# The first four products as one group, x past column 512 and the norm weights turned by VectorE and DRAM, and every block exchange in GpSimd's queue

## The chip, the cores and the metric

The kernel runs on one core of one Trainium2 chip. The metric is the device time of one execution in microseconds (us); lower is better. A core has TensorE (PE; its loading of the stationary operand is shown apart as PEld), VectorE (DVE), ScalarE (ACT), GpSimd (POOL) and SyncE (SP). Each engine works through its own instructions in order and waits for others by semaphores. DMAs are issued from the queues of SP, ACT or POOL, and share 16 DMA engines.

## What is computed

One decoder layer on 256 tokens of width 2048, in float32: a SwiGLU half, a token mixer of attention and a gated spatial branch, and a second SwiGLU half, each on the RMS-normed residual stream.

```python
x = x + 1/2 * swiglu(rmsnorm(x, ffn1_norm), ffn1_w_gate, ffn1_w_up, ffn1_w_down)
x = x + hybrid_mixer(rmsnorm(x, mix_norm), w_in, ...)
x = x + 1/2 * swiglu(rmsnorm(x, ffn2_norm), ffn2_w_gate, ffn2_w_up, ffn2_w_down)
return rmsnorm(x, final_norm)
...
def swiglu(x, w_gate, w_up, w_down):
    return (jax.nn.silu(x @ w_gate) * (x @ w_up)) @ w_down
```

The weights are read once: 2048 x 5632 for gate, up and down of each FFN, 2048 x 11776 for `w_in`, and three smaller ones.

## The kernel before

**Products.** Every matrix product is cut into columns of 512 (`NC`). A `gemm` is one such column block: 256 tokens (two tiles `t` of 128) by 512 columns, summed over `nk` blocks of 128 rows of the weight. Its two sums stand in two PSUM banks. Precision comes from splitting both operands in two float32r parts: the stationary side is `xhi` and `xlo` (transposed activations, 128 rows of the width by 256 tokens), the moving side is `wh` and `wl`. For each block of 128 rows and each `t` three products are made: wh by xhi ("hh"), wl by xhi ("hl"), wh by xlo ("lh").

**Units.** Weights come in units of four row blocks (1 MB, tile `raw`, three buffers), loaded by SP. A unit is two half units; the list `hus` holds all half units in the order of work, and the loop at the end runs through it by an index `i`. For each half unit ScalarE copies `raw` to `wh` (line 139) and VectorE subtracts to get `wl` (line 140); both have four buffers, so the splits of half unit `i` + 4 wait for TensorE to finish `i`. A half unit is 12 products on TensorE (line 149). `at(i, fn)` puts other work behind the products of half unit `i`, ahead of the splits of the half units that follow. So the order on every engine is written out by this loop.

**Order of half units.** `lay_out` takes the gemms one after the other; where a gemm has `pair`, it and the next one are interleaved so that the last unit of each comes at the end.

**The start.** x (256 x 2048) is not normed ahead: the products use x times the norm's weight, and 1/rms of each token is applied to the results. TensorE transposes x, 128 columns `k` at a time (`first_transposes`, line 235, two transposes each), ScalarE and VectorE evacuate it, scaled by the norm's weight, to `xhi` and `xlo` (`first_evac`, lines 239 and 240). This happens between the products of the first gemm, two `k` for each half unit ahead, laid out by hand in `begin`, `ready`, `early` and `midway`. SP loads x in five pieces between the first weights. The norm weights come as rows (`rows`), and TensorE transposes them to columns (`gcols`): the first 16 at the start, the other 44 at half unit 60 (`gains`).

**Block exchanges.** Everywhere else a transpose is done by `turn`: VectorE transposes blocks of 32 x 32 (`blocks`, line 191 or 197), one DMA writes 512 KB to DRAM (line 175), three half units later four DMAs of 128 KB read the blocks back, permuted (`back`, line 181), and `lag` (six or eight) half units after the first step the result is evacuated (`ev`). All five DMAs stand in SP's queue, between the weight loads. There are 49 such exchanges: the hidden activations of both FFNs, x after the first two parts of the layer, and those of the mixer.

Of the kernel before, what the change touches and what calls it, by code (L numbers as in the profile page):

```python
# [16 lines left out]
P = 128  # L17
S = 256
NT = S // P
# [22 lines left out]
def layer(ctx: ExitStack, tc: tile.TileContext, a, out):  # L42
# [25 lines left out]
    rows = sb.tile([60, P], F32, name="rows")  # L68
# [6 lines left out]
    load_rows(0, ACT)  # L75
    half = sb.tile([P, 2], F32, name="half")
# [3 lines left out]
    junk = sb.tile([P, NC], BF16, name="junk")  # L80
    DVE.memset(junk, 0.0)
# [12 lines left out]
    gcols = sb.tile([P, 60], F32, name="gcols")  # L94
# [6 lines left out]
    def gemm(w, c0, rows0, nk, lhs, post, pair=False):  # L101
        gemms.append(dict(w=w, c0=c0, rows0=rows0, nk=nk, lhs=lhs, post=post, pair=pair))


    def lay_out():
        i = 0
        while i < len(gemms):
            gs = gemms[i:i + 2] if gemms[i]["pair"] else gemms[i:i + 1]
            i += len(gs)
            units = [(g, u) for g in gs for u in range(g["nk"] // UK)]  # L110
            if len(gs) == 2:
                units.sort(key=lambda q: q[1] == q[0]["nk"] // UK - 1)
            for g, u in units:
                hus.extend([(g, u, 0), (g, u, 1)])
# [5 lines left out]

    def load_unit(i, parts=(0, 4)):
        g, u, _ = hus[2 * i]
        if i in raws:
            r = raws[i]
        else:
            r = raws[i] = big.tile([P, UK, NC], F32, tag="raw", bufs=RAWB, name=f"raw{i}")
        k0 = g["rows0"] + u * UK * P
        src = g["w"][k0:k0 + UK * P, g["c0"]:g["c0"] + NC].rearrange("(k p) c -> p k c", p=P)
        k = slice(*parts)
        SP.dma_start(r[:, k], src[:, k])  # L130
# [12 lines left out]
    def product(i, jj, t, kind):  # L143
        g, u, j = hus[i]
        if "ps" not in g:
            g["ps"] = [mm_bank(f"mm{i}_{q}") for q in range(NT)]
# [21 lines left out]
    def turn(i, name, q, put, dst, ev, lag=8):  # L168
        got = {}

        def blocks():
# [3 lines left out]
            SP.dma_start(m, d.rearrange("p j m b -> p j (m b)"))  # L175

        def back():
            got["e"] = e = dst()
            m = got["m"].rearrange("(i a) j r -> j a i r", a=32)
            for j in range(4):  # L180
                SP.dma_start(e[32 * j:32 * j + 32].rearrange("p (i r) -> p i r", i=4), m[j])

        at(i, blocks)
        at(i + 3, back)
# [47 lines left out]
    def first_transposes(k):  # L232
        b = first_banks[k] = first_banks.get(k) or tp_bank(f"xt{k}")
# [8 lines left out]
    def residual(e, n, c, banks, scale, norm):  # L242
# [16 lines left out]

        def evac(src):  # L260
# [7 lines left out]
        turn(e + (6 if c == 1 else 2), f"x{n}_{c}", 8, put_tokens(lambda: x[:, :, cs]),  # L268
# [537 lines left out]
    def ready(i, whole=False):  # L806
# [7 lines left out]
        if whole:  # L814
            split(i)
# [90 lines left out]
```

## Time and profile before

| | us |
|---|---|
| median of 3 runs | 2047.57 (2047.5 to 2048.29) |
| the profiled execution | 2047.7 |
| its span in the trace | 2046.0 |
| TensorE busy | 2035.8 |
| ScalarE busy | 974.5 |
| VectorE busy | 1182.3 |
| GpSimd busy | 12.5 |

Times in the trace count from the start of the span. The waits of an engine are given with what ended them; a DMA's time is from its issue to its landing. Matmuls are pipelined, so a product's own 0.38 us overlaps the next one; what counts is the distance from start to start. Lines of the kernel are named L and a number.

### The profile page before, as it was taken

The page shows a single profiled execution, that of the slowest core. Times are in us where ns is not written, and L with a number is a line of the kernel's source. Part 1 is how long each engine was busy: PE and PEld are TensorE (multiplying, and loading weights), DVE is VectorE, ACT ScalarE, POOL GpSimd, SP SyncE. Part 2 cuts the span into 40 slices and gives each one's busy share as a digit, 9 for nine tenths or more (in the row PEclk, how much of TensorE's full clock was granted, in tenths as well). Part 3 has the DMA queues.
Part 4 walks back from the last instruction along what each step waited for, and adds up shares of the span by engine and source line. Part 5 has one row for each costly group of instructions (what it writes and reads, how often), then busy time and mean ns, then how long its engine had stood idle before and what let it go on. Part 6 is the DMA issues. An engine that isn't in the chain of part 4 may idle for free.

```text
span 2046.0 us, 23823 instructions
## 1 busy us (share of the span) xinstructions
PE 2035.8 (100%) x9494; PEld 1781.4 (87%) x9494; DVE 1182.3 (58%) x1193; ACT 974.5 (48%) x1071; POOL 12.5 (1%) x18
## 2 busy tenths in 40 slices
PE   9999999999999999999999999999999999999998
PEld 7888888888888888888888888888888888888887
DVE  5555555455555657665665555565555555555554
ACT  6444444444445555455554444564444444444443
POOL 0000000000000000000000000000000000000000
PEclk9999999999999999999999999999999999999999
DMA  7776876566766855787766666776676656667664
GB/s 271 234 236 226 270 245 216 201 223 225 243 231 217 269 201 202 241 276 261 261 222 220 224 225 206 246 256 231 221 242 224 225 206 205 224 222 240 231 214 144
DMA packets 246775, 469.35 MB, mean 229 GB/s; under 512 B 11084, under 2 KB 38536, under 8 KB 246536
## 3 DMA queue, kind: packets, MB, share of 16 engines
q1 hardware_dynamic: 246344, 467.30, 68.8%
q8 instruction: 74, 1.21, 0.2%
q10 hardware_dynamic: 320, 0.53, 0.1%
q14 instruction: 37, 0.30, 0.0%
HBM read 439.22 MB, written 28.57 MB: 229 GB/s over the span
## 4 chain that ended last, share of the span: by engine, by line
PE 99%; issue 0%; ACT 0%; DVE 0%; POOLq 0%; POOL 0%
PE mm L149 98%; PE sp L458 0%; PE warm L772 0%; PE pv L624 0%; PE sc L587 0%; PE xt L235 0%; PE sc L585 0%; PE pv L620 0%; ACT x L740 0%; ACT xhi L239 0%; PE pv L621 0%; DVE x L725 0%; POOLq L901 0%; POOL rf L732 0%; ACT wh L139 0%
## 5 line engine op out<-in xcount | busy, mean ns | idle before, releaser
L140 DVE TENSOR_TENSOR wl<-raw,wh 128x1024 fp32r<-128x1024 f32 (+1 forms) x780 | 947.6, 1218 | 822.7 <-ACT wh L139 817.6
L139 ACT ACTIVATE wh<-raw 128x1024 fp32r<-128x1024 f32 (+1 forms) x780 | 817.9, 1052 | 1007.6 <-PE mm L149 976.7
L149 PE MATMUL mm<-wh,xhi 128*128 128x512 f32 x2144 | 814.0, 380 | 0.5 <-ACT wh L139 0.4
L149 PE MATMUL mm<-wh,xlo 128*128 128x512 f32 x2144 | 812.5, 379 | 0.0
L149 PE MATMUL mm<-wl,xhi 128*128 128x512 f32 x2144 | 811.8, 379 | 0.0
L149 PEld LDWEIGHTS mm<-wh,xhi 128*128 128x128 f32 x2144 | 405.2, 189 | 58.6 <-ACT wh L139 0.9
L149 PEld LDWEIGHTS mm<-wl,xhi 128*128 128x128 f32 x2144 | 405.4, 189 | 57.3
L149 PEld LDWEIGHTS mm<-wh,xlo 128*128 128x128 f32 x2144 | 405.2, 189 | 57.4
L149 PE MATMUL mm<-wl,hhi 128*128 128x512 f32 x704 | 266.8, 379 | 0.0
L149 PE MATMUL mm<-wh,hhi 128*128 128x512 f32 x704 | 266.8, 379 | 0.0
L149 PE MATMUL mm<-wh,hlo 128*128 128x512 f32 x704 | 266.8, 379 | 0.0
L149 PEld LDWEIGHTS mm<-wl,hhi 128*128 128x128 f32 x704 | 133.1, 189 | 18.9
L149 PEld LDWEIGHTS mm<-wh,hlo 128*128 128x128 f32 x704 | 133.1, 189 | 18.9
L149 PEld LDWEIGHTS mm<-wh,hhi 128*128 128x128 f32 x704 | 133.1, 189 | 18.9
L149 PE MATMUL mm<-wh,uT 128*128 128x512 f32 x192 | 58.0, 379 | 0.0
L149 PE MATMUL mm<-wh,mhi 128*128 128x512 f32 x128 | 48.5, 379 | 0.0
L149 PE MATMUL mm<-wl,mhi 128*128 128x512 f32 x128 | 48.5, 379 | 0.0
L149 PE MATMUL mm<-wh,mlo 128*128 128x512 f32 x128 | 48.5, 379 | 0.0
L149 PEld LDWEIGHTS mm<-wh,uT 128*128 128x128 f32 x192 | 36.3, 189 | 5.1
L149 PE MATMUL mm<-wl,uT 128*128 128x512 f32 x96 | 36.4, 379 | 0.0
L304 DVE SCALAR_TENSOR_TENSOR sg<-mm,rstd,sg 128x512 f32<-128x512 f32 x44 | 30.9, 743 | 0.0
L219 ACT ACTIVATE junk<-x 128x512 bf16<-128x512 f32 x30 | 18.9, 629 | 25.0 <-DVE x L247 18.6
(152 smaller groups left out, 600.6 us busy)
## 6 DMA issues: line engine op xcount, KB each, us to landing
raw<-in_w_in_dram SPq DMA_DIRECT2D x92, 1024.0 KB, 5.0
raw<-in_ffn_w_up_dram SPq DMA_DIRECT2D x88, 1024.0 KB, 5.1
raw<-in_ffn_w_down_dram SPq DMA_DIRECT2D x88, 1024.0 KB, 5.1
raw<-in_ffn_w_gate_dram SPq DMA_DIRECT2D x84, 1024.0 KB, 5.0
raw<-in_w_out_dram SPq DMA_DIRECT2D x16, 1024.0 KB, 5.1
raw<-in_w_sg_out_dram SPq DMA_DIRECT2D x12, 1024.0 KB, 5.7
bmh<-bth SPq DMA_DIRECT2D x22, 512.0 KB, 2.7
sg<-bmh SPq DMA_DIRECT2D x88, 128.0 KB, 4.9
```

The source lines that it names most:

```text
L139: ACT.activation(wh[:, k], r[:, k], AF.Copy)
L140: DVE.tensor_tensor(wl[:, k], r[:, k], wh[:, k].bitcast(F32), op=OP.subtract)
L149: PE.matmul(g["ps"][t], act[:, k, t * P:(t + 1) * P], in_turn(w[:, jj]), start=k == 0 and kind == "hh", stop=k == g["nk"] - 1 and kind == ...
L219: ACT.activation(junk, x[:, t, c * NC:(c + 1) * NC], AF.Square, accum_out=ss[n][:, t, c:c + 1])
L304: DVE.scalar_tensor_tensor(two(sg[:, t]), banks[t], rstd[:, t:t + 1], two(sg[:, t]), op0=OP.mult, op1=OP.mult)
```

## The change

Four edits go together.

1. **Order of the first four gemms.** `lay_out` now takes groups with bounds. The first four gemms (gate and up of the first two column blocks) are interleaved: half unit 0 of each (x columns 0 to 255), then half unit 1 of each (256 to 511), then half units 2 and 3 of each (512 to 1023), then the rest. Their eight sums stand in all eight banks of PSUM. A raw unit may now hold parts of two gemms.
2. **x past column 512.** TensorE transposes only `k` 0 to 3. The other three parts of 512 columns (`c` = 1, 2, 3) go through `turn`, at half units 1, 7 and 8. The last two loads of x are put off to half units 3 and 4.
3. **Norm weights.** The other 44 rows (and the biases in them) are transposed by VectorE in blocks and exchanged over DRAM by SP, at half units 32, 36 and 40.
4. **Block exchanges.** All five DMAs of every `turn` are issued from GpSimd's queue.

```diff
-    def turn(i, name, q, put, dst, ev, lag=8):
+    def turn(i, name, q, put, dst, ev, lag=8, read=3):
...
-            SP.dma_start(m, d.rearrange("p j m b -> p j (m b)"))
+            POOL.dma_start(m, d.rearrange("p j m b -> p j (m b)"))
...
-                SP.dma_start(e[32 * j:32 * j + 32].rearrange("p (i r) -> p i r", i=4), m[j])
+                POOL.dma_start(e[32 * j:32 * j + 32].rearrange("p (i r) -> p i r", i=4), m[j])
...
-        at(i + 3, back)
+        at(i + read, back)
...
+            steps = [(g, q) for g in gemms[i:i + size] for q in range(g["nk"] // 2)]
+            i += size
+            steps.sort(key=lambda s: sum(s[1] >= (b if b > 0 else s[0]["nk"] // 2 + b) for b in bounds))
+            hus.extend((g, q // 2, q % 2) for g, q in steps)
+
+    PAIR = (2, (-2,))
+    FIRST = (4, (1, 2, 4))
...
-    ffn(a["ffn1_w_gate"][0], a["ffn1_w_up"][0], a["ffn1_w_down"][0], down1, False)
+    ffn(a["ffn1_w_gate"][0], a["ffn1_w_up"][0], a["ffn1_w_down"][0], down1, FIRST)
...
-    load_unit(0, (1, 2))
+    for k in (1, 2, 3):
+        load_unit(0, (k, k + 1))
     load_x(S, NC)
-    load_unit(0, (2, 3))
-    load_unit(0, (3, 4))
-    for c in range(1, 4):
-        load_x(c * NC, (c + 1) * NC)
-        load_unit(c, (0, 2))
-        load_unit(c, (2, 4))
+    for k in (0, 1):
+        load_unit(1, (k, k + 1))
+    load_x(NC, 2 * NC)
+    for k in (2, 3):
+        load_unit(1, (k, k + 1))
+    load_unit(2)
...
-    def gains():
-        b = tp_bank("gc1")
-        PE.transpose(b[:, 0:60], rows, ident[0:60, 0:60])
-        DVE.tensor_copy(gcols[:, 16:60], b[:, 16:60])
...
+    def more_rows():
+        POOL.memset(rows[32:64], 0.0)
+        for i in range(1, 4):
+            load_rows(i)
+
+    def rows_out():
+        d = sb.tile([64, P], F32, name="gd")
+        DVE.transpose(d.rearrange("p (j b) -> p j b", b=32), rows.rearrange("p (j b) -> p j b", b=32))
+        xT["gains"] = m = dram.tile([64, P], F32, name="gm")
+        SP.dma_start(m, d)
+
+    def rows_back():
+        m = xT["gains"].rearrange("(i a) (j b) -> j a i b", a=32, b=32)
+        for j in range(4):
+            SP.dma_start(gcols[32 * j:32 * j + 32].rearrange("p (i b) -> p i b", i=2), m[j])
...
+    for c, i, lag, read in ((1, 1, 3, 1), (2, 7, 5, 3), (3, 8, 5, 3)):
+        turn_x(i, 0, c, lag, read)
+    for c in (2, 3):
+        at(c + 1, lambda c=c: load_x(c * NC, (c + 1) * NC))
...
+    split(0, slice(0, 1))
+    first_x((0, 1))
+    for i, k in ((0, 1), (1, 0), (1, 1), (2, 0), (2, 1)):
+        split(i, slice(k, k + 1))
     for i in range(n):
...
+        if i < n - LA - 1:
+            products(i, jjs=(0,), high_first=i < 4)
+            if i == 1:
+                first_x((2, 3))
+            products(i, jjs=(1,), high_first=i < 4)
         for f in callbacks.pop(i, []):
             f()
-        if i > 4:
-            advance(i + LA + 2)
+        if i > 0:
+            advance(i + LA + (2 if i > 1 else 0))
```

`turn_x` holds what `residual` did before: four scalings by the norm's weight on ScalarE (line 264 before, 273 now), one copy to `xhi`, and VectorE's subtraction to `xlo`.

On TensorE, before, in the second half unit of the program (mm0 is the first gemm, xt4 and xt5 the transposes of x columns 512 to 767):

```order
L149 MATMUL mm0_1_139<-wh1_161,xhi0_118 128x512
L149 MATMUL mm0_1_139<-wh1_161,xlo0_119 128x512
L149 MATMUL mm0_0_138<-wl1_162,xhi0_118 128x512
L149 MATMUL mm0_1_139<-wl1_162,xhi0_118 128x512
L235 MATMUL xt4_173<-ident_76,x_81 128x128 x2
L235 MATMUL xt5_176<-ident_76,x_81 128x128 x2
L149 MATMUL mm0_0_138<-wh1_161,xhi0_118 128x512
L149 MATMUL mm0_0_138<-wh1_161,xlo0_119 128x512
```

And now, in the second half unit, which belongs to the second gemm (mm1):

```order
L155 MATMUL mm1_1_161<-wl1_135,xhi0_115 128x512
L241 MATMUL xt2_168<-ident_76,x_81 128x128 x2
L241 MATMUL xt3_171<-ident_76,x_81 128x128 x2
L155 MATMUL mm1_0_160<-wh1_134,xhi0_115 128x512
L155 MATMUL mm1_0_160<-wh1_134,xlo0_116 128x512
L155 MATMUL mm1_1_161<-wh1_134,xhi0_115 128x512
```

These are the last transposes of x on TensorE now; before, five more such places follow.

On ScalarE, before, around the split of half unit 8 (wh8):

```order
L239 ACTIVATE xhi0_118<-xt15_292,gcols_84 128x256
L139 ACTIVATE wh7_299<-raw3_103 128x1024
L139 ACTIVATE wh8_321<-raw4_315 128x1024
L139 ACTIVATE wh9_325<-raw4_315 128x1024
L139 ACTIVATE wh10_343<-raw5_317 128x1024
```

And now; xt0_1 is the block of x columns 512 to 1023 read back from DRAM:

```order
L145 ACTIVATE wh7_246<-raw3_189 128x1024
L273 ACTIVATE xt0_1_210<-xt0_1_210,gcols_84 128x2x4x32 x4
L169 ACTIVATE xhi0_115<-xt0_1_210 128x1024
L145 ACTIVATE wh8_271<-raw4_215 128x1024
L145 ACTIVATE wh9_287<-raw4_215 128x1024
```

The evacuation of the exchanged block stands between the splits of half units 7 and 8.

On GpSimd, whose first work after the start was the power for the first norm (line 226 before), there stand now ahead of it:

```order
L181 DMA bmx0_1_187<-btx0_1_184 128x1024
L187 DMA xt0_1_210<-bmx0_1_187 32x4x256 x4
L181 DMA bmx0_2_324<-btx0_2_321 128x1024
L181 DMA bmx0_3_347<-btx0_3_344 128x1024
L187 DMA xt0_2_387<-bmx0_2_324 32x4x256 x4
L187 DMA xt0_3_412<-bmx0_3_347 32x4x256 x4
L232 TENSOR_TENSOR rstd0_436<-ms0_433,half_72 128x2
```

Before, none of its instructions was a DMA; now it issues 260.

More of the change, by code (lines that the diff above doesn't have):

```diff
@@ L75, in layer @@
     load_rows(0, ACT)
+    junk = sb.tile([P, NC], BF16, name="junk")
+    DVE.memset(junk, 0.0)
     half = sb.tile([P, 2], F32, name="half")
@@ L107, in lay_out @@
         while i < len(gemms):
[L108 to L114, printed above, removed]
+            size, bounds = gemms[i]["group"]
+            steps = [(g, q) for g in gemms[i:i + size] for q in range(g["nk"] // 2)]
[4 more added lines that the diff above has]
+    FIRST = (4, (1, 2, 4))
     def at(i, fn):
```

102 lines of the change are left out of this document (35 added, 67 removed).

## The prediction

> **What bounds the kernel now.** I read the page's busy times first, then its costliest groups, then the table of waits of TensorE, then the timeline of the first 25 us.
>
> ```profile
> span 2046.0 us, 23823 instructions
> PE 2035.8 (100%) x9494; PEld 1781.4 (87%) x9494; DVE 1182.3 (58%) x1193; ACT 974.5 (48%) x1071; POOL 12.5 (1%) x18
> ...
> PE 99%; issue 0%; ACT 0%; DVE 0%; POOLq 0%; POOL 0%
> ...
> L140 DVE TENSOR_TENSOR wl<-raw,wh 128x1024 fp32r<-128x1024 f32 (+1 forms) x780 | 947.6, 1218 | 822.7 <-ACT wh L139 817.6
> L139 ACT ACTIVATE wh<-raw 128x1024 fp32r<-128x1024 f32 (+1 forms) x780 | 817.9, 1052 | 1007.6 <-PE mm L149 976.7
> ```
> ```profile
> PE warm L772 <- DVE junk L81: 1.3, 1, 1.3
> PE mm L149 <- ACT wh L139: 0.4, 1, 0.4
> ```
>
> The chain that ended last is 99% TensorE. TensorE's own waits are two, 1.3 us before anything is there and 0.4 us once. ScalarE, in contrast, waits 976.7 us for TensorE to give a buffer back. So from about 25 us to the end nothing but the count of products sets the time, and only the start, an instruction more or less on TensorE, or a new wait can move it. The profiled execution took 2047.7 us, 1.7 us around its span, and stands 0.13 us above the median of 2047.57.
>
> ```profile
> 6.23 0.79 PE L149 MATMUL mm<-wh,xhi 128*128 128x512 f32 x1
> 7.20 0.63 ACT L139 ACTIVATE wh<-raw 128x512 fp32r<-128x512 f32 x1 [0.59 <-DMA raw<-in_ffn_w_gate_dram]
> 9.29 0.59 PE L149 MATMUL mm<-wl,xhi 128*128 128x512 f32 x2
> 10.25 0.48 PE L149 MATMUL mm<-wh,xhi 128*128 128x512 f32 x1 [0.36 <-ACT wh L139]
> 10.57 0.38 PE L149 MATMUL mm<-wh,xlo 128*128 128x512 f32 x1
> 11.21 0.59 PE L149 MATMUL mm<-wl,xhi 128*128 128x512 f32 x2
> 11.65 0.60 PE L235 MATMUL xt<-ident,x 128*128 128x128 f32 x4
> 12.00 0.46 PE L149 MATMUL mm<-wh,xhi 128*128 128x512 f32 x1
> 12.30 0.38 PE L149 MATMUL mm<-wh,xlo 128*128 128x512 f32 x1
> 30.04 0.38 PE L149 MATMUL mm<-wl,xhi 128*128 128x512 f32 x1
> 44.93 0.38 PE L149 MATMUL mm<-wl,xhi 128*128 128x512 f32 x1
> 168.17 0.38 PE L149 MATMUL mm<-wh,xlo 128*128 128x512 f32 x1
> 168.48 0.27 PE L785 MATMUL gc<-ident,rows 60*128 60x60 f32 x1
> 168.68 0.48 PE L149 MATMUL mm<-wh,xhi 128*128 128x512 f32 x1
> 169.00 0.38 PE L149 MATMUL mm<-wl,xhi 128*128 128x512 f32 x1
> ```
>
> Between 30.04 and 44.93 stand 69 products, 0.216 us each: that is the pace.
>
> **What is removed.** One visit of TensorE to four transposes: after two products from 11.21 the second next would start at 11.21 + 3 x 0.216 = 11.86; it starts at 12.30, so a visit costs **0.44 us**. Before there are seven visits after the first product, for x columns 256 to 2047; the order keeps the first of them (the same 256 columns, in the second half unit) and drops six: 6 x 0.44 = 2.64. The wait at 10.25: two products from 9.29 would be followed at 9.72 and 9.94, and the second came at 10.57: **0.63**. It comes because ScalarE has to evacuate x and split weights in turn; now four half units use the same 128-column blocks 0 and 1, and their weights' splits stand ahead of the next evacuation. The transposes of the norm weights: two products behind 168.17 would bring 168.60; it was 169.00: **0.40**. Their replacement (a 64-row transpose by VectorE, five small DMAs, a memset) lies at half units 32 to 40 behind VectorE's 822.7 us of idle time, and its result is used at the end of the first FFN, over 400 us later: 0. Without waits: 2047.7 - 2.64 - 0.63 - 0.40 = **2044.0**.
>
> The first product stays at 6.23: the first three loads are the same. The memset of junk goes ahead of two of 0.06 us: 0 to 0.1 gained, taken as 0. The loads that follow are the same bytes in an order nearer to their use, half of what x asked for is put off, and half unit 3 (due at about 15) sees its low part between 0.4 us early and 0.5 late: taken as 0.
>
> **What is added: the first block exchange, c = 1.** Half unit 8 is the first to use x columns 512 to 1023. It starts 90 products after the one that stood at 7.94 before, plus one visit: 7.94 + 19.4 + 0.5 = 27.9; its second product needs wl8, at 28.1. What must come before:
>
> ```profile
> GB/s 0 14 262 286 211 195 268 368 406 397 412 401 408 408 410 410 406 412 401 412 401 399 100 182 406 389 51 33 276 399 414 406 403 164 49 205 408 360 29 20
> L191 DVE STREAM_TRANSPOSE btx<-x 128x512 f32<-128x512 f32 x16 | 10.4, 687 | 0.0
> L239 ACT ACTIVATE xhi<-xt,gcols 128x256 fp32r<-128x256 f32 x16 | 7.0, 471 | 6.1 <-PE xt L235 6.1
> L264 ACT ACTIVATE xt<-xt,gcols 128x256 f32<-128x256 f32 x32 | 13.5, 494 | 1.3 <-DMA xt<-bmx 1.3
> L163 ACT ACTIVATE xhi<-xt 128x1024 fp32r<-128x1024 f32 x8 | 8.5, 1058 | 0.3
> L164 DVE TENSOR_TENSOR xlo<-xt,xhi 128x1024 fp32r<-128x1024 f32 x8 | 9.8, 1225 | 13.1 <-ACT xhi L163 13.1
> ```
> ```profile
> bmx<-btx SPq DMA_DIRECT2D x8, 512.0 KB, 2.8
> xt<-bmx SPq DMA_DIRECT2D x32, 128.0 KB, 4.8
> bmp<-btp SPq DMA_DIRECT2D x4, 512.0 KB, 4.1
> p<-bmp SPq DMA_DIRECT2D x16, 128.0 KB, 6.8
> k<-bmk SPq DMA_DIRECT2D x12, 128.0 KB, 8.0
> ```
> ```profile
> 648.50 1.75 SPq L181 DMA_DIRECT2D xt<-bmx  x4
> L226 POOL TENSOR_TENSOR rstd<-ms,half 128x2 f32<-128x2 f32 x3 | 2.1, 701 | 995.9 <-DVE ms L224 995.9
> L393 POOL TENSOR_TENSOR lnrs<-ve,half 128x2 f32<-128x2 f32 x1 | 1.6, 1595 | 60.7 <-DVE ve L391 60.7
> ```
>
> Each number of the first row is one us. The third load ends at 0.79 MB, moved by 5.1, and ScalarE began on it at 7.20, 2.1 later; the first load (0.26 MB) was moved by 2.9 and used at 3.7; I take 1.4 for the lag. Step by step: the second part of wh2 is the eighth piece (2.1 MB, moved by 9.2), lands at 10.6 and is split by 11.2; two evacuations of 0.47 on ScalarE, and VectorE's half of the last, bring 12.7; x columns 512 to 1023 (2.6 MB) are there at 11.9; two transposes of 0.687 end at **14.1**. Then one write of 512 KB to DRAM and four reads back, now issued by GpSimd. Then ScalarE, whose queue waits there with wh8 behind it: 4 x 0.494 + 1.058 for the block, 1.05 for wh8; VectorE does xlo (1.225), then wl8 (1.22). With T the last landing, wl8 is ready at T + 3.03 + 1.23 + 1.22 = T + 5.5. So the wait is **T - 22.6**, where positive.
>
> No row shows a DMA of GpSimd's. At SP's quiet prices the write takes 2.8, the fourth read is issued 1.3 after the first (1.75 for four) and lands 4.8 later: T = 14.1 + 2.8 + 1.3 + 4.8 = 23.0, a wait of 0.4. At the prices of the attention part's exchanges, 4.1 and 8.0: T = 27.5, wait 4.9. The first us row says which is nearer: 10 to 21 us moves 400 GB/s and more throughout, as full as any part, but GpSimd's queue has nothing queued ahead, where SP's had weights. I take the middle of the quiet and the busy prices (2.8 and 4.1; 4.8 and 6.8), T = 24.65. GpSimd's issue of one DMA I bound from 0.44 (SP's) to 1.6 (the dearer of its two-element operations) and take 1.0, not far from the 0.70 row; it adds 0.6 to the write and up to 1.7 to the reads, half of it beside transfers: 1.1. T = 25.8 and the wait is **3.2**, bounds 0 to 8.
>
> A rule that speaks against this edit: the Trainium skill, "DMA: Bandwidth & Descriptors", section "Latency and other measured facts", gives 0.6 us to the first byte for DMAs of SP and ScalarE and about 1 us for GpSimd's. No row here shows GpSimd's. By that rule T would be an estimated 0.8 later over the two legs, and the sum below 2049.3.
>
> **The second and third exchange, c = 2 and 3.** They are due at half units 16 and 18, the first of them 20.7 us after half unit 8, at 51.8. VectorE transposes them behind the splits of half units 10 and 11 (wl8 at 31.3, 1.22 for each split, 1.4 for each pair), done at 35.1 and 37.7. By the middle prices each takes 11.7 from there (25.8 - 14.1): c = 2 lands at 46.8, c = 3, whose reads stand behind those of c = 2, at about 51. ScalarE has 3.03 for c = 2, 1.05 for wh16, 3.03 for c = 3 and 1.05 for wh17, in this order; with VectorE's 1.23 and 1.22 behind each, wl16 is there at 52.3 (due 52.0) and wl17 at 56.5 (due 54.9): waits of 0.3 and 1.6. By the quiet prices both are in time, by the busy ones the two cost 3. The first row above has gaps from 22 us on (100, 51, 33, 164, 49), so this place is nearer to quiet than half unit 8 is; I take **1.3**, bounds 0 to 3.
>
> **The other 49 exchanges, moved from SP's queue to GpSimd's.** In SP's queue they held back weight loads; but the waits that this made ended at ScalarE, not at TensorE:
>
> ```profile
> ACT wh L139 <- DMA raw<-in_w_in_dram: 15.9, 9, 3.3
> ACT pTk L607 <- DMA p<-bmp: 0.9, 1, 0.9
> ```
>
> So nothing is won. Lost is nothing as long as the block arrives in its lag of six or eight half units (15.5 or 20.7 us) against 2.8 + 1.3 + 4.8 = 8.9; behind a waiting DMA on GpSimd stand only the next exchanges and the two-element powers for the norms, needed later. Taken as 0.
>
> **Sum:** 2044.0 + 3.2 + 1.3 = **2048.5 us**.
>
> **Rivals.** (A) All three exchanges come in time, since the queue of their own spares them the weights: T below 22.6, no wait, **2044.0**. For it speaks the wait of 0.4 at quiet prices, against it the 400 GB/s beside it. (B) Slower: an exchange by GpSimd costs more than SP's dearest. If each issue takes 1.6 and the landings are those of k<-bmk, T = 14.1 + 5.3 + 4.8 + 8.0 = 32.2, a wait of 9.6 at half unit 8, and of 3 at 16 and 17: 2044.0 + 12.6 = **2056.6**. It decides from waits of 3.7 on (all that is saved) and is measurable from 7.8 on. In such a wait TensorE is idle for long, and this case has a row of its slow pace, seven warm-up products in 3.17 us, 0.45 each where 0.216 is usual:
>
> ```profile
> 1.32 3.17 PE L772 MATMUL warm<-junk 128*128 128x512 bf16 x7 [1.32 <-DVE junk L81]
> ```
>
> The Trainium skill, "TensorE: Matmul & The Clock Gate", section "Part 1: The HAM clock gate", says that an idle window of about 3.4 us halves the clock until one busy window has passed. By that rule B would cost an estimated 1.7 us more (half of 3.4), 2058.3, and the forecast nothing, its wait being in parts (for wh8, then for wl8) that are shorter. (C) The move of the late exchanges does cost: the four of the attention part have no slack on ScalarE (the 0.9 above). Some 3 us more for each would reach TensorE's product with pT for about 1.5 each, 6 in all: **2054.5**. Against it: only those four are that tight.
>
> **How the numbers follow.** Forecast 0.5 (2045.5 to 2051.7), A 0.2, B 0.22, C 0.08. About 0.2%, 4.1 us, is what a measurement here can tell from no change. All that can be saved, 3.7, is less than that, so faster has 0.04 (A with the small gains at the start); the slower side is B, C and the edge of the forecast, 0.30; the same is 0.66. The range goes from A, 2044.0, to 2055, which leaves out the dear half of B.
>
> **What would show it.** Six visits fewer and no wait of TensorE before 27 us; at half unit 8 a wait of TensorE that ends with wl, with ScalarE waiting for the landing of xt; smaller ones at 16 and 17; the products otherwise 0.216 apart. Wrong would be: TensorE waiting earlier (weights late), no wait at all (A), or waits after 70 us (C).

## The result, and the profile after

The changed kernel takes **2060.56 us** (median of 6 runs, 2057.63 to 2062.73), the kernel before 2047.54 beside it: a ratio of **1.006**, 95% interval 1.0049 to 1.007. It is 13 us slower; the forecast was 2048.5, the range ended at 2055. The profiled execution took 2058.45, so it lies 2 us below the median, and its sum is made against the 2047.7 of before: 10.7 us to explain. The other 2 us of the median are not in this profile; what the runs show of them stands with e12.

Of the page after, the span, the shares of the chain that ended last, and TensorE's two groups of products with their idle time:

```profile
span 2056.6 us, 23906 instructions
...
PE 64%; DMA 2%; issue 1%; ACT 1%; DVE 1%; POOL 0%; POOLq 0%; ACTq 0%; DVEq 0%
...
L155 PE MATMUL mm<-wh,xhi 128*128 128x512 f32 x2144 | 814.6, 380 | 6.1 <-ACT wh L145 5.7
L155 PE MATMUL mm<-wl,xhi 128*128 128x512 f32 x2144 | 813.0, 380 | 3.9 <-DVE wl L146 3.9
```

TensorE waits 5.7 us for ScalarE's split and 3.9 for VectorE's, about 10 in all. Where they are is seen when the products are numbered: at the usual pace product N starts (N - 1) x 0.2158 us behind the first one. The start of product N, counted from the start of the span, less (N - 1) x 0.2158 is the time lost so far; it holds the time ahead of the first product too (6.23 us before, 5.87 after). Product 97 is the first of half unit 8, 145 the first of half unit 12, 300 the last of half unit 24. For the two kernels, in us:

| lost by product | 72 | 97 | 145 | 300 | 2900 | 3300 | 4000 |
|---|---|---|---|---|---|---|---|
| before | 10.40 | 10.40 | 10.40 | 10.41 | 10.89 | 10.91 | 15.17 |
| after | 6.90 | 11.85 | 15.63 | 19.33 | 19.42 | 20.98 | 25.86 |

(Between 3300 and 4000 other work of TensorE stands; it makes 4.26 before.) So the new order is 3.50 ahead at product 72, where 3.27 was forecast (2.64 + 0.63); 0.36 of the 3.50 is the earlier first product. Then 4.95 go at product 97, 3.78 up to product 145, 3.70 up to product 300 (all but 0.2 of it in three waits at half units 16 and 17), and 1.5 and 0.6 behind product 2900, at 700 to 735 us. The norm weights' 0.4 (10.41 to 10.89 before) are saved. In sum, from the unrounded starts, -3.50 + 4.95 + 3.78 + 3.70 - 0.39 + 1.54 + 0.62 = 10.7.

TensorE's timeline at half unit 8 (start, busy us, the wait in brackets), and the windows around it (busy us of PE, PEld, DVE, ACT and POOL with their counts, granted clock, share of the DMA engines, GB/s):

```profile
27.40 0.38 PE L155 MATMUL mm<-wh,xlo 128*128 128x512 f32 x1
32.57 0.80 PE L155 MATMUL mm<-wh,xhi 128*128 128x512 f32 x1 [4.79 <-ACT wh L145]
34.02 0.79 PE L155 MATMUL mm<-wl,xhi 128*128 128x512 f32 x1 [0.65 <-DVE wl L146]
34.60 0.63 PE L155 MATMUL mm<-wh,xlo 128*128 128x512 f32 x1
35.03 0.63 PE L155 MATMUL mm<-wh,xhi 128*128 128x512 f32 x1
```
```profile
30.00:32.00 2.00, 0.00 (x0) 0.00 (x0) 0.40 (x1) 1.97 (x4) 0.00 (x0) 1.00 0.61 238
32.00:34.00 2.00, 0.80 (x1) 0.29 (x1) 2.00 (x3) 2.00 (x3) 0.00 (x0) 0.54 0.02 8
...
36.00:38.00 2.00, 2.00 (x6) 1.56 (x5) 2.00 (x4) 0.72 (x2) 0.26 (x1) 0.50 0.80 203
38.00:40.00 2.00, 2.00 (x8) 1.68 (x7) 1.77 (x3) 0.89 (x1) 0.30 (x1) 0.75 1.07 422
40.00:42.00 2.00, 2.00 (x11) 1.74 (x10) 1.23 (x1) 1.78 (x6) 0.55 (x1) 1.00 0.90 330
```

The wait is 5.17 - 0.22 = 4.95 from product to product, then 1.45 - 0.22 = 1.23 for wl8. The granted clock is 0.5 from 32.2 to 39.0, and the products behind the waits stand 0.43 apart until 38.9: 2.55 more by product 145. What ScalarE and GpSimd did meanwhile, from their timelines:

```profile
28.78 1.70 ACT L273 ACTIVATE xt<-xt,gcols 128x256 f32<-128x256 f32 x4 [9.51 <-DMA xt<-bmx]
30.51 1.06 ACT L169 ACTIVATE xhi<-xt 128x1024 fp32r<-128x1024 f32 x1
31.47 3.88 ACT L145 ACTIVATE wh<-raw 128x1024 fp32r<-128x1024 f32 x4
...
53.17 1.71 ACT L273 ACTIVATE xt<-xt,gcols 128x256 f32<-128x256 f32 x4 [5.21 <-DMA xt<-bmx]
...
58.23 1.70 ACT L273 ACTIVATE xt<-xt,gcols 128x256 f32<-128x256 f32 x4 [1.31 <-DMA xt<-bmx]
```
```profile
14.07 0.73 POOL L181 DMA_DIRECT2D bmx<-btx  x1 [12.69 <-DVE btx L197]
19.73 2.19 POOL L187 DMA_DIRECT2D xt<-bmx  x4 [4.93 <-DMA bmx<-btx]
37.74 0.56 POOL L181 DMA_DIRECT2D bmx<-btx  x1 [15.82 <-DVE btx L197]
40.06 0.55 POOL L181 DMA_DIRECT2D bmx<-btx  x1 [1.76 <-DVE btx L197]
42.25 2.23 POOL L187 DMA_DIRECT2D xt<-bmx  x4 [1.63 <-DMA bmx<-btx]
50.11 2.22 POOL L187 DMA_DIRECT2D xt<-bmx  x4 [5.63 <-DMA bmx<-btx]
```

ScalarE's queue stands at the first evacuation for 9.51 us, with the splits of half units 8 to 11 behind it, all ready to run (3.88 us without a gap afterwards). The exchange begins when forecast, at 14.07, but its write lands 5.36 later and the last of its reads 7.30 behind its issue at 21.37: T = 28.67. The third exchange's write takes 9.37. In the first write's time, seen by DMA queue (packets, MB, share of 16 engines; q0 is GpSimd's, q1 SP's):

```profile
DMA packets 1024, 2.23 MB, mean 406 GB/s; under 512 B 62, under 2 KB 62, under 8 KB 1024
## 3 DMA queue, kind: packets, MB, share of 16 engines
q1 hardware_dynamic: 880, 1.71, 80.7%
q0 software_dynamic: 144, 0.52, 23.3%
```

The engines are full. The quarter that the exchange has of them is a mean of two parts: by the same view, from 14.1 to 16.3 no packet of q0 moves (q1 0.90 MB, 407 GB/s), and from 16.3 to 19 q0 has 47.4% of the engines and moves its 0.52 MB. The reads, issued from 19.73 on, are the same: no packet from 19.7 to 23.4 (q1 1.47 MB, 402 GB/s in all), then 0.52 MB by 28.7. The first packets start at 16.4 and 23.5, so some 6 of the 14.6 us are time in which nothing of the exchange moves while SP's loads do. Why they come so late isn't settled: beside 382 GB/s, reads issued at 658.5 had their first packet 1.5 us later. Of the 22 exchanges of the FFNs' hidden activations, in stretches of some 200 to 270 GB/s, the median write of the same 512 KB takes 3.3 in GpSimd's queue (2.7 in SP's before), and an issue is 0.55 us:

```profile
L187 POOL DMA_DIRECT2D sg<-bmh x88 | 48.6, 553 | 80.4 <-DMA bmh<-bth 71.0
...
bmh<-bth POOLq DMA_DIRECT2D x22, 512.0 KB, 3.3
sg<-bmh POOLq DMA_DIRECT2D x88, 128.0 KB, 4.1
```

### The profile page after: what moved, and what is told of

It reads as the page before. It is cut to its first block, busy times and chain, and to the rows that moved or that the text cites. A ratio compares the mean times of both kernels' runs of the same rounds, so it can differ in the third digit from the quotient of the medians.

```text
span 2056.6 us, 23906 instructions
## 1 busy us (share of the span) xinstructions
PE 2037.0 (99%) x9469; PEld 1779.9 (87%) x9469; DVE 1183.6 (58%) x1189; ACT 977.6 (48%) x1073; POOL 158.0 (8%) x279
## 4 chain that ended last, share of the span: by engine, by line
PE 64%; DMA 2%; issue 1%; ACT 1%; DVE 1%; POOL 0%; POOLq 0%; ACTq 0%; DVEq 0%
PE mm L155 63%; DMA xt<-bmx 1%; DMA bmx<-btx 1%; POOL xt L187 0%; DVE wl L146 0%; ACT xt L273 0%; PE sp L468 0%; PE pv L634 0%; PE sc L597 0%; ACT xhi L169 0%; PE sc L595 0%; DVE xlo L170 0%; PE pv L630 0%; ACT x L750 0%; DVE btx L197 0%
## 5 line engine op out<-in xcount | busy, mean ns | idle before, releaser
L181 POOL DMA_DIRECT2D bmh<-bth x22 | 12.4, 564 | 905.9 <-DVE bth L197 905.9
L187 POOL DMA_DIRECT2D sg<-bmh x88 | 48.6, 553 | 80.4 <-DMA bmh<-bth 71.0
L170 DVE TENSOR_TENSOR xlo<-xt,xhi 128x1024 fp32r<-128x1024 f32 x11 | 13.5, 1225 | 48.9 <-ACT xhi L169 48.9
```

Of the source, the lines that this page charges most:

```text
L170: DVE.tensor_tensor(lo, src, hi.bitcast(F32), op=OP.subtract)
L181: POOL.dma_start(m, d.rearrange("p j m b -> p j (m b)"))
L187: POOL.dma_start(e[32 * j:32 * j + 32].rearrange("p (i r) -> p i r", i=4), m[j])
```

## The experiments

The theory: the new order of products is the gain that it was thought to be, and all of the loss is exchanges that land after their evacuation is due on ScalarE, because they stand beside weight loads that SP's queue would have held back. Rivals: the new start itself is too tight, in any queue; GpSimd's queue is slow in itself; the slow clock is what costs. All kernels in one table, with the time lost by product as above (the fillers of e4 not counted); the ratio is to the kernel before, timed on the same chip.

| kernel | median us (runs) | ratio, 95% interval | 72 | 97 | 145 | 300 | 2900 | 3300 |
|---|---|---|---|---|---|---|---|---|
| e1 after, all on SP | 2054.54 (6) | 1.0021 to 1.0045 | 8.83 | 8.83 | 9.56 | 17.80 | 17.89 | 17.90 |
| e2 before, 49 on GpSimd | 2051.64 (10) | 1.0013 to 1.0031 | 10.13 | 10.13 | 10.14 | 10.14 | 10.62 | 12.45 |
| e3 after, evacuation later | 2056.14 (4) | 1.0027 to 1.006 | 6.73 | 10.49 | 12.95 | 13.20 | 13.29 | 15.24 |
| e4 after, filler | 2061.13 (4) | 1.0053 to 1.0083 | 6.90 | 12.77 | 13.39 | 20.11 | 20.19 | 22.55 |
| e5 after, 49 on SP | 2057.75 (4) | 1.0031 to 1.0061 | 7.02 | 11.72 | 15.93 | 21.11 | 21.20 | 21.21 |
| e6 slack, all on SP | 2051.80 (10) | 1.0007 to 1.0026 | 7.02 | 9.94 | 11.84 | 11.84 | 11.93 | 11.94 |
| e7 slack, first three on GpSimd | 2051.61 (10) | 1.0009 to 1.0028 | 6.54 | 10.44 | 12.59 | 12.60 | 12.69 | 12.70 |
| e8 as e2, evacuation later | 2047.41 (10) | 0.9988 to 1.0007 | 10.14 | 10.14 | 10.14 | 10.15 | 10.63 | 10.64 |
| e9 no first exchange | 2048.87 (11) | 0.9993 to 1.001 | 10.43 | 10.43 | 10.43 | 10.44 | 10.52 | 10.54 |
| e10 after, x loads later | 2063.20 (4) | 1.0056 to 1.0088 | 6.52 | 11.81 | 15.25 | 21.77 | 21.86 | 25.83 |
| e11 slack, all on GpSimd | 2050.57 (10) | 1.0002 to 1.0021 | 7.03 | 10.84 | 13.46 | 13.47 | 13.55 | 13.57 |
| e12 after again | 2058.47 (4) | 1.0041 to 1.0072 | 7.03 | 11.19 | 13.99 | 17.53 | 17.62 | 18.96 |
| e13 as e9, second visit later | 2046.22 (11) | 0.9985 to 1.0002 | 9.32 | 9.32 | 9.32 | 9.33 | 9.41 | 9.43 |
| e14 as e13, more warm-up | 2046.19 (11) | 0.9984 to 1.0001 | 8.97 | 8.97 | 8.97 | 8.98 | 9.07 | 9.08 |
| e15 as e13, visits earlier | 2044.99 (11) | 0.9977 to 0.9996 | 7.91 | 7.91 | 7.91 | 7.91 | 8.00 | 8.01 |

### e1: the changed kernel, all exchanges back in SP's queue

```diff
-            POOL.dma_start(m, d.rearrange("p j m b -> p j (m b)"))
+            SP.dma_start(m, d.rearrange("p j m b -> p j (m b)"))
...
-                POOL.dma_start(e[32 * j:32 * j + 32].rearrange("p (i r) -> p i r", i=4), m[j])
+                SP.dma_start(e[32 * j:32 * j + 32].rearrange("p (i r) -> p i r", i=4), m[j])
```

> The changed kernel, with all 52 exchanges back in SP's queue; the new start stays. Theory Q (the exchanges are late because on a queue of their own they share the DMA engines with weight loads that SP's queue would have held back): the write of the first exchange lands in about 2.8 us and the reads in about 5, T near 23 to 24, a wait at half unit 8 below 2 us, no slow pace of TensorE, no waits at 705 and 733 us: 2044 to 2047 us. Theory S (the start is too tight in either queue, since VectorE's transposes end at 14.1): the wait at half unit 8 stays above 4 us, or SP's waits make weights late before 27 us: 2054 us or more.

Half of theory Q came. SP's queue (timeline), ScalarE at the first evacuation, and TensorE at the later one:

```profile
15.32 0.34 SPq L181 DMA_DIRECT2D bmx<-btx  x1
...
18.45 1.76 SPq L187 DMA_DIRECT2D xt<-bmx  x4
```
```profile
25.14 1.70 ACT L273 ACTIVATE xt<-xt,gcols 128x256 f32<-128x256 f32 x4 [1.65 <-DMA xt<-bmx]
```
```profile
57.53 0.48 PE L155 MATMUL mm<-wh,xhi 128*128 128x512 f32 x1 [2.10 <-ACT wh L145]
```

The write lands 3.07 behind its issue (5.36 on GpSimd's queue) and the whole exchange takes 9.7 in place of 14.6, since SP issues the weights only behind it: 0.71 MB were moved in all from 15.3 to 18.5, against 2.23 in 5.5 us above. Half unit 8 loses 0.7, and the waits behind product 2900 go. But the second and third exchange are late here too (evacuated from 47.5 and 53.7; their writes, with weight loads ahead of them in SP's queue, took 5.7 and 4.6 us) and cost 8.2 us, a slow pace included. So the queue is a part, not the whole. The median, 2054.54, lies where theory S put it, but neither sign of S came: the wait at half unit 8 is short, and TensorE doesn't wait before 27 us. (In this run the first products stood 0.43 apart until 10.3 us, which is the 1.9 more at product 72.)

### e2 and e8: the 49 exchanges alone, and the slack that they need

e2 is the kernel before with only the queue changed, the same two lines as in e1 the other way round; e8 is e2 with one number more:

```diff
-        turn(e + (6 if c == 1 else 2), f"x{n}_{c}", 8, ..., evac, 6)
+        turn(e + (6 if c == 1 else 2), f"x{n}_{c}", 8, ..., evac, 8)
```

> The kernel before, with its 49 exchanges in GpSimd's queue and nothing else changed. Theory Q: the queue alone costs the waits seen at 705 and 733 us in the changed kernel, about 2 us: 2048.5 to 2051 us, the start as before. Theory N (the late exchanges cost nothing, as predicted; those two waits come from the shifted order): 2047 to 2048 us. If the queue is the dear part of the whole change: 2054 us or more.

> The kernel before with its 49 exchanges in GpSimd's queue, and the evacuation of the x exchanges 8 half units behind their start in place of 6. Landings stay as late as on GpSimd's queue with 6. Theory W (the cost is ScalarE's queue standing at an evacuation whose block has not landed, with splits behind it): the waits at 697 and 725 us go, 2047 to 2048.5 us. Rival (the load on the DMA engines itself costs, through late weights): 2050 to 2052 us as with 6.

e2 is 4.2 us slower than before, a little more than expected (3.2 in its profile, all of it at two places of TensorE, 697 and 725 us); e8 isn't slower at all. ScalarE's evacuations of x in the mixer's norm, in e2 and then in e8:

```profile
693.57 1.70 ACT L264 ACTIVATE xt<-xt,gcols 128x256 f32<-128x256 f32 x4 [4.49 <-DMA xt<-bmx]
...
721.14 1.71 ACT L264 ACTIVATE xt<-xt,gcols 128x256 f32<-128x256 f32 x4 [5.65 <-DMA xt<-bmx]
```
```profile
692.86 1.69 ACT L264 ACTIVATE xt<-xt,gcols 128x256 f32<-128x256 f32 x4
...
718.98 1.69 ACT L264 ACTIVATE xt<-xt,gcols 128x256 f32<-128x256 f32 x4
```

The last of these exchanges took 13.8 us in e2 from the issue of its write (707.22) to its last landing (721.04), and 13.3 in e8 (704.25 to 717.52). This transfer is nearly as slow in e8 (the one before it took 11.3 in place of 13.3); what went is the place in ScalarE's queue where splits had to stand behind it. The load on the DMA engines alone costs nothing here.

### e5: the changed kernel, only the first three exchanges on GpSimd's queue

```diff
         got = {}
+        queue = POOL if name[:3] == "x0_" else SP
```

> The changed kernel with GpSimd's queue for the first three exchanges only; the other 49 back in SP's. Theory Q (the 49 cost 3 to 4 us, as they did in the kernel before): the waits behind 690 us go, the start stays as in the changed kernel (a wait of about 6 us at half unit 8, slow pace, waits at 16 and 17): 2060.6 - 4 = 2056.5 us, within 1.5. Rival (the 49 were dear only with the old start): 2059 us or more. If all of the loss came from the 49: about 2047.

The loss at 700 to 735 us is gone (21.20 to 21.21 between products 2900 and 3300), and so is 2.8 of the median, a little less than expected; the start is at least as bad as in the changed kernel (21.11 lost by product 300 in place of 19.33, with the clock at 0.5 a second time, from 63.6 to 67.0).

### e3: the first evacuation two half units later

```diff
-    for c, i, lag, read in ((1, 1, 3, 1), (2, 7, 5, 3), (3, 8, 5, 3)):
+    for c, i, lag, read in ((1, 1, 5, 1), (2, 7, 5, 3), (3, 8, 5, 3)):
```

> The changed kernel, with the evacuation of the first exchange two half units later in the queues, so that the splits of half units 8 and 9 stand ahead of it on ScalarE and VectorE. T stays at about 28.7. Theory W (the wait is T plus what stands on the two engines behind the landing): half unit 8 starts at T + 2.8 = 31.5 in place of 32.6 and the second wait of 1.2 us goes: 2.3 us less, the slow pace stays since TensorE is still idle for 4 us: about 2056 (profile) to 2058 (median). Rival: wait falls below what slows TensorE and another 2.6 us go: 2053.5. Rival: the DMA is all that counts and nothing changes.

T stays (28.26), the time falls by 4.4. At half unit 8 TensorE now waits for the block itself:

```profile
31.21 0.48 PE L155 MATMUL mm<-wh,xhi 128*128 128x512 f32 x1 [3.60 <-ACT xhi L169]
31.53 0.38 PE L155 MATMUL mm<-wl,xhi 128*128 128x512 f32 x1
32.47 0.79 PE L155 MATMUL mm<-wh,xlo 128*128 128x512 f32 x1 [0.56 <-DVE xlo L170]
```

The loss between products 72 and 145 falls from 8.73 to 6.22, by 2.5 where 2.3 was expected, but not by the expected parts alone: half unit 8 starts 1.2 earlier relative to the pace (1.1 expected), the second wait falls by 0.5 (1.2 expected), and the slow pace, expected to stay, costs 0.8 less, since the clock is at 0.5 for 3.4 us in place of 6.8. The last part can be chance: see e12. More is won behind it: the transposes of the second exchange stand on VectorE behind the splits of half units 8 to 10, so its write goes out at 35.06 in place of 37.74, and half units 16 to 20 lose 0.25 in place of 3.70. One late landing makes the next.

### e4: products of zeros in the wait

```diff
+            if i == 8:
+                bank = hus[8][0]["ps"][0]
+                for _ in range(28):
+                    PE.matmul(bank, junk[:, 0:P], junk, start=False, stop=False)
```

> The changed kernel, with 28 products of zeros (6 us of TensorE) ahead of half unit 8, added into a running sum. TensorE is busy while it would wait. Theory C (after a long idle time TensorE runs at half pace for 5 us, 10 products at 0.43 in place of 0.216): the landing and the start of half unit 8 stay within 0.3 us, the granted clock stays 1.0, the products behind are 0.216 apart and the time falls by up to 2.6 us. Rival (the pace is hidden by the splits of half units 8 to 11, which keep ScalarE and VectorE fully busy until 36 us): waits for wl take its place, and the time falls by less than 1 us.

The clock holds (windows), the next products are at full pace, and the time is the same, 2061.13; TensorE's timeline shows where it goes:

```profile
32.00:34.00 2.00, 2.00 (x10) 0.83 (x8) 2.00 (x2) 2.00 (x3) 0.00 (x0) 1.00 0.04 14
34.00:36.00 2.00, 1.84 (x9) 1.60 (x9) 2.00 (x3) 2.00 (x4) 0.00 (x0) 1.00 0.00 0
```
```profile
34.75 0.38 PE L155 MATMUL mm<-wh,xhi 128*128 128x512 f32 x1
34.97 0.38 PE L155 MATMUL mm<-wl,xhi 128*128 128x512 f32 x1
...
61.24 0.48 PE L155 MATMUL mm<-wh,xhi 128*128 128x512 f32 x1 [1.42 <-ACT wh L145]
62.68 0.80 PE L155 MATMUL mm<-wl,xhi 128*128 128x512 f32 x1 [0.96 <-DVE wl L146]
```

By product 145 the kernel is 2.2 ahead of the changed one; by product 300 it is 0.8 behind. The second exchange lands at 51.8, only 1.2 earlier than in the changed kernel, and TensorE is there 2.2 earlier: four waits at half units 16 and 17 make 4.9 where three made 3.5, and behind the last of them the slow pace comes after all, for 1.6. The fillers also end late: half unit 8 starts at 33.49 in place of 32.57, and the wait for wl8 falls from 1.23 to 0.51. So both theories fail here: the clock's 2.2 us were won, and given back at the next landing.

### e10: less beside the first exchange?

```diff
-        at(c + 1, lambda c=c: load_x(c * NC, (c + 1) * NC))
+        at(5, lambda c=c: load_x(c * NC, (c + 1) * NC))
```

> The changed kernel, with the loads of x columns 1024 to 2047 (1 MB, first used at 36 us) one weight load later in SP's queue. Theory D (the first exchange is late because its packets share some 400 GB/s with everything SP has issued): 1 MB less stands beside the reads for about 2.5 us, T goes from 28.7 to between 26.5 and 28 and the wait at half unit 8 falls with it: 1 to 2 us less, 2058.5 to 2060. Rival G (GpSimd's queue itself is slow, its landings do not depend on what else moves): T stays within 0.3 us and the time within 1 us of 2060.6. Rival: the weights take the room that x leaves (the 1 MB that is moved ahead is as large), and T does not move either.

T = 28.63: it doesn't move. The weight load that changed places with x is as large, so the run doesn't tell late packets beside full engines from a slow queue. e1, and the 3.3 us of the same write in a quiet stretch, speak against the slow queue. The median, 2063.20, is above all that was expected: half units 16 to 20 lose 6.5 in place of 3.7, the mixer's norm 4.0 in place of 1.6, and behind both the clock is at 0.5 once more.

### e6, e7, e11: slack for all three exchanges

Three kernels with these two edits; all exchanges in SP's queue (e6), the 49 in SP's (e7), or all in GpSimd's and `lag` 8 as in e8 (e11).

```diff
-    FIRST = (4, (1, 2, 4))
+    FIRST = (4, (1, 2, 4, 6))
...
-    for c, i, lag, read in ((1, 1, 3, 1), (2, 7, 5, 3), (3, 8, 5, 3)):
+    for c, i, lag, read in ((1, 1, 5, 1), (2, 7, 7, 3), (3, 8, 11, 3)):
```

> The changed kernel with three edits that give the landings time: all exchanges in SP's queue; evacuations of the first three 2, 2 and 6 half units later, so that splits stand ahead of them; a bound more in the first group, so that the third exchange is needed at half unit 24 in place of 18. Theory W (only landings that come too late cost, and the new order of products is itself a gain of 3.5 us): no wait of TensorE from 12 to 100 us above 1 us, the time 2044 to 2046 us, below before. Rival S (the slow clock of the first products, 10.3 us in the run on SP's queue against 5.9 before, belongs to the new order): 2047 to 2049.

> As the one before it, but with GpSimd's queue for the first three exchanges, SP's for the others. Theory Q+W: T of the first exchange stays near 28.7, so a wait of about 3.5 us stays at half unit 8, with the slow pace or without it, and the other two exchanges cost nothing: 2048 to 2051 us. If GpSimd's queue is harmless once there is slack: equal to the one before it within 1 us.

> The changed kernel with all its exchanges and queues, only with slack: evacuations of the first three 2, 2 and 6 half units later, the third needed at half unit 24, the x exchanges of the later norms with 8 half units. Theory W: only the wait for the first exchange is left, 3.5 us at half unit 8 and the slow pace behind it, 1.5 to 2.5: 2047.6 - 3.9 + 5.5 = 2049.2 us, between 2048 and 2050.5, with no waits from 100 us on. Rival: waits elsewhere take their place, 2051 or more.

The second and third exchange cost nothing in any of them (the columns 145 and 300 agree), nor do the later 49 in e11. What is left is half unit 8: 6.4 us in e11 (1.9 of it slow pace), 6.1 in e7 (1.4), and 4.8 in e6. So e6 misses its range by 6 us; e7, 2051.61, and e11, 2050.57, end just above theirs. In e6 the block is there early and the weights aren't; ScalarE's timeline:

```profile
25.92 2.00 ACT L145 ACTIVATE wh<-raw 128x1024 fp32r<-128x1024 f32 x2 [3.51 <-DMA raw<-in_ffn_w_gate_dram]
27.83 1.69 ACT L273 ACTIVATE xt<-xt,gcols 128x256 f32<-128x256 f32 x4
```

SP's queue gives the exchange the bandwidth and takes it from the weights; GpSimd's does it the other way round. From 10 to 24 us the engines move some 400 GB/s, and 1 MB more of exchange has to come from somewhere. (e6 loses some 3 us more at 870 to 885 us, where ScalarE waits for weights, 16.7 us in six waits, and e7 0.8; this wasn't followed up.)

### e9, e13, e15: TensorE turns the first of the three parts after all

If the first exchange can't be in time, it has to go. All eight banks are taken from half unit 3 on; so the fourth gemm begins at half unit 6, and one bank is free until then for x columns 512 to 1023. All other exchanges stay in GpSimd's queue, with the slack of e11. The core of it:

```diff
+            if size == 4:
+                steps[0:8] = [steps[k] for k in (0, 1, 2, 4, 5, 6, 3, 7)]
...
-        b = first_banks[k] = tp_bank(f"xt{k}")
+        b = tp_bank(f"xt{k}") if k < 4 else first_banks["spare"]
+        b = first_banks[k] = b[:, (k % 2) * S * (k > 3):]
...
-    for c, i, lag, read in ((1, 1, 3, 1), (2, 7, 5, 3), (3, 8, 5, 3)):
+    for c, i, lag, read in ((2, 7, 7, 3), (3, 8, 11, 3)):
...
             if i == 1:
                 first_x((2, 3))
+                first_banks["spare"] = tp_bank("xt4")
+            if i in (3, 4):
+                first_x((2 * i - 2, 2 * i - 1))
```

e13 moves the second visit behind half unit 4, e15 both: the first to the middle of half unit 2, the second behind half unit 3.

> The first exchange is taken out: x columns 512 to 1023 are turned by TensorE, in half units 3 and 4, through a PSUM bank that is still free because the fourth product of the group now starts at half unit 6 in place of 3. The second and third exchange stay in GpSimd's queue, with their evacuations later and the third needed at half unit 24; all exchanges stay in GpSimd's queue, those of x with 8 half units. Theory W: no wait at half unit 8; the two visits of TensorE cost 0.9 us of the 3.5 gained; nothing else is lost: 2047.6 - 3.5 + 0.9 - 0.4 = 2044.6 us, between 2043.5 and 2046. Rival (weights are the next to be late, since 400 GB/s are in use until 25 us): waits of ScalarE for raw turn into waits of TensorE before 30 us, 2047 or more.

> As the kernel in which TensorE turns x columns 512 to 1023, with the second of its visits behind half unit 4 in place of in its middle, so that it doesn't wait for the bank (0.5 us there). With the release of the clock at 4.5 to 6.9: 2047.4 - 2.0 - 0.5 = 2045 us; with a release at 10.3: 2047. The median tells which is the more usual: below 2046, or 2047 and above as the 2048.9 of the kernel it is made from.

> As e13, with the two visits of TensorE in the middle of half unit 2 and behind half unit 3, so that the first evacuation stands ahead of the splits of half units 4 to 6. If the wait of 1.2 us came from the order in ScalarE's queue, it goes and nothing takes its place: 2046.2 - 1.2 = 2045.0 us, between 2044.6 and 2045.6, the kernel before at 2047.6. Rival (the weights that come at 17.7 us are the bound there, with 400 GB/s in use): TensorE waits for the splits of half units 4 to 6 instead, 2046 us or more.

No wait at half unit 8 is left in any of them. e9 is no faster than before and misses its range (2043.5 to 2046); its profiled run, 2047.40, has the slow first products of e1 (1.9 us). Its eleven runs fall in two groups, five of 2047.2 to 2047.9 and six of 2048.9 to 2049.6, and what parts them wasn't settled. e13, 2046.22, lies between its two forecasts: the slow first products are not there, but the second visit waits for the bank longer than in e9 (1.19 in place of 0.46), and the bank waits for an evacuation behind a split whose weights come at 17.9 (ScalarE, then TensorE):

```profile
17.98 1.06 ACT L147 ACTIVATE wh<-raw 128x1024 fp32r<-128x1024 f32 x1 [1.50 <-DMA raw<-in_ffn_w_up_dram]
18.95 0.46 ACT L248 ACTIVATE xhi<-xt,gcols 128x256 fp32r<-128x256 f32 x1
20.73 0.47 ACT L248 ACTIVATE xhi<-xt,gcols 128x256 fp32r<-128x256 f32 x1 [1.32 <-DVE xlo L249]
```
```profile
21.77 0.66 PE L244 MATMUL xt<-ident,x 128*128 128x128 f32 x4 [1.19 <-DVE xlo L249]
```

With the evacuation ahead of that split the wait goes and nothing takes its place. e15's visits on TensorE:

```profile
13.50 0.60 PE L244 MATMUL xt<-ident,x 128*128 128x128 f32 x4
...
17.82 0.60 PE L244 MATMUL xt<-ident,x 128*128 128x128 f32 x4
```

**e15 beats both kernels**: 2044.99 us against 2047.87 of before beside it, ratio 0.9986 (0.9977 to 0.9996), as expected. (The changed kernel was timed on other chips: 2060.56 and, in e12, 2058.47.)

### e12 and e14: the spread

> The changed kernel again, nothing edited, for a second profile and more times. If the late release of TensorE's clock (10.3 in place of 4.5 to 6.9 us) makes the median stand 2.1 us above the first profile, a profiled run near 2060.5 shows it. Rival (the landings of the second and third exchange vary from run to run): the start as in the first profile, and other waits from 55 to 65 us.

> As the one before it, with three warm-up products in place of one behind the transposition of the norm weights: the first product comes up to 0.9 us later. Theory H (a window of TensorE's first 7 us is just too empty in some runs, and the clock stays slow for 3.4 us more): no run keeps the slow pace until 10 us, the spread falls below 1 us, 2045 to 2046.5. Rival (the phase alone decides, not how busy the window is): the same spread, 0.4 to 0.9 us later.

e12 is the changed kernel unedited. Its second profile starts as the first; it loses 1.8 us less between products 72 and 145, and 0.2 less at half units 16 to 20, where the third exchange's write took 7.2 us in place of 9.4. Of the 1.8, 0.8 is the earlier landing (T is 28.0, the first wait 4.16 in place of 4.95), and 1.0 is the clock, which is at 0.5 for 3.4 us in place of 6.8 (windows, as above):

```profile
34.00:36.00 2.00, 2.00 (x6) 1.62 (x5) 2.00 (x3) 1.97 (x5) 0.00 (x0) 0.50 0.23 28
36.00:38.00 2.00, 2.00 (x10) 1.71 (x9) 2.00 (x4) 0.56 (x2) 0.56 (x1) 0.91 0.80 279
```

So both the landings and the length of the slow pace make a part of the spread (2057.0 to 2062.7 over its 10 runs, median 2059.8; so what e3 and e5 win against it is some 0.8 less than against the first median). e14 (`keep_warm(3)` for `keep_warm(1)`) is as fast as e13 and spreads as little; since no run of e13 is slow by 1.9 us, the longer warm-up had nothing to show. What holds the slow pace until 10.3 us in e1 and e9, and how often, stays open.

## Why the prediction was wrong

From the forecast to the profiled run: 2048.5 + 3.0 (half unit 8) + 2.55 (the slow clock behind it) + 2.4 (the second and third exchange) + 2.2 (the 49 others) - 0.2 (the saving) = 2058.4. One by one:

**The saving was right.** Six visits, the wait at 10.25 and the norm weights were put at 3.67; measured are 3.50 and 0.39 in the first profile, 3.37 and 0.4 in e12. Of the 3.50, 0.36 is luck: the first product came at 5.87, where the prediction kept it at 6.23 (in e12 it came at 6.18). e15, with two visits more, keeps 2.49 and 0.39 of it, and with no late landing that is what its time shows.

**The wait formula was right, T was not.** Wait = T - 22.6 gives 6.1 for T = 28.67; the two waits of TensorE were 4.95 + 1.23 = 6.2. The step that failed is the choice of T: 10 to 21 us "moves 400 GB/s and more throughout, as full as any part, but GpSimd's queue has nothing queued ahead", and so the middle of the quiet and the busy prices. GpSimd's queue did have nothing ahead, and it didn't help: the first packets moved 2.4 us behind the issue of the write and 3.8 behind that of the first read, while SP's loads moved 400 GB/s. The sum had 3.45 for the write, 1.3 from the first to the fourth read, 5.8 for the reads and 1.1 for slower issues, 11.65; it took 5.66 to the first read, 1.64 to the fourth and 7.30 to its landing, 14.60. An issue was put too high (1.0, measured 0.55). Even the busy price (T = 27.5) was too low. The Trainium skill, "DMA: Bandwidth & Descriptors", section "Latency and other measured facts", gives about 1 us to the first byte for DMAs of GpSimd and 0.6 for those of SP, 0.4 apart. The quiet writes here are 0.6 apart (3.3 against 2.7), a small part of the 2.9 us by which T was off.

**The second and third exchange: 1.3 forecast, 3.7 measured.** The step took "this place is nearer to quiet", with 11.7 us from the transposes to the landing. That span was 15.6 for the second (37.44 to 53.02), and the transposes ended 2.3 later than worked out, behind splits that had waited for the first exchange. Where the first us row of before had gaps, the changed kernel moves 203 to 422 GB/s in each 2 us from 36 to 56 (three of these windows stand above): a place's load was read from a trace whose start the change itself replaces.

**The slow clock: nothing forecast, 2.55 measured.** The prediction left it out of the sum, since the forecast wait was short; for a wait as in rival B it had an estimate of 1.7 us. The case came and cost more: the granted clock was 0.5 for 6.8 us. The Trainium skill, "TensorE: Matmul & The Clock Gate", section "Part 1: The HAM clock gate", has the slow state end after one busy window of some 3.4 us. The traces of e3, e6, e7, e11 and e12 agree, with 3.4 us at 0.5 around the start of half unit 8; that of the changed kernel, with 6.8, doesn't, nor do those of e5 and e10. e4, where it was kept away, was no faster, since the next landing was the bound.

**The 49 others: "taken as 0", measured 2.2 in the changed kernel and 4.2 in e2.** The step compared a lag of 15.5 us with 2.8 + 1.3 + 4.8 = 8.9, from SP's quiet prices. Both sides were off. From issue to landing it was 13.8 for the worst in e2, and the slack was not 15.5: ScalarE stood ready 8.3 us behind the issue of that write, and 8.9 behind that of the one before. Line L264 of the prediction's own rows showed it: before the change, ScalarE already waited 1.3 us for a block, which took 10.5 us in SP's queue. Rival C had the kind (late exchanges) but not the place: in e2 the four of the attention part cost nothing, the exchanges of x in the mixer's norm all of it.

**The rivals.** B, 2056.6 or 2058.3 with the clock, was nearest, and its kind is what the runs show: a dear first exchange and the slow clock behind it, with T between the forecast's 25.8 and its own 32.2. Its prices for the write and the last read (5.3 and 8.0) were near (5.66 and 7.30); its 4.8 for issues was not (1.64). That its sum comes so near is in part luck: it had 9.6 at half unit 8, where 6.2 were measured, and nothing for the 49 others. It was given 0.22, and its dear half was left out of the range.

## What to carry to other kernels

Here a queue of its own didn't make a transfer faster while SP's loads kept the DMA engines full (5.36 us for the first write, 3.07 in SP's order): it took away the order in which one gave way to the other. Price a new transfer by what moves beside it at that time, not by the same transfer's row in a quiet stretch. And before moving transfers to a slower queue, look at what stands behind their consumer in its engine's queue: placing the evacuation of the x exchanges two half units later gave back all of the 4.2 us that the queue had cost the kernel before.

## Hardware behaviour that was not expected

- The granted clock fell to 0.5 in a wait of 4.95 us, and also in e6, where TensorE was idle for 2.76 us (0.5 from 30.5 to 33.9). Three waits within 7 us at 57 to 64 (1.14, 1.12 and 1.23) left it at 1.00 in the changed kernel; in e5 three waits at the same place (0.69, 1.36 and 1.23) brought it to 0.5 for 3.4 us. What decides is not shown.
- With 1.71 MB of loads from SP's queue beside it a write of 512 KB from GpSimd's queue took 5.36 us, 2.4 of them ahead of its first packet; the third exchange's, with the second's reads beside it as well, took 9.37, and the same write 3.3 in a quiet stretch.
- In two of the kernels with the new start the first products ran at half pace until 10.3 us; in the others the trace has the full clock from a point between 4.1 and 7.3 us on, with the same instructions on TensorE up to there (but for the longer warm-up of e14).
